# A transformer trunk on one Trainium2 core: the token sums of the seven-product pairs traced earlier, their bank evacuations at high priority, and another division of the scratch buffers

## The chip, the core and the metric

The kernel runs on one core of a Trainium2 chip. The engines that matter here are TensorE (PE: matmuls, with its weight loads PEld), VectorE (DVE), ScalarE (ACT), GpSimd (POOL) and SyncE (SP), whose queue starts nearly all transfers. Each engine works through its own instructions in a fixed order and waits on semaphores for the others. The metric is the device time of one execution in microseconds (us), lower being better.

## What is computed

Two layers run over 256 tokens of width 1024, in fp32. Each layer is a feed-forward block, a mixer (differential attention beside an mLSTM) and another feed-forward block, each with RMSNorm before and after. So there are four feed-forward passes, here called pass 1 to 4.

```python
def _swiglu(h, w_in, w_out):
    gate, up = jnp.split(h @ w_in, 2, axis=-1)
    return (jax.nn.silu(gate) * up) @ w_out

def reference(x, ffn_w_in, ffn_w_out, norm_gains, mix_w_in, mix_w_out, da_lambda, ...):
    for l in range(DEPTH):
        g = norm_gains[l]
        h = _swiglu(_rmsnorm(x, g[0]), ffn_w_in[l, 0], ffn_w_out[l, 0])
        x = x + 0.5 * _rmsnorm(h, g[1])
        lam_init = 0.8 - 0.6 * math.exp(-0.3 * l)
        h = _mixer(_rmsnorm(x, g[2]), mix_w_in[l], mix_w_out[l], da_lambda[l], da_subln_g[l],
                   lam_init, ml_conv_w[l], ml_conv_b[l], ml_gate_b[l], ml_norm_g[l])
        x = x + _rmsnorm(h, g[3])
        h = _swiglu(_rmsnorm(x, g[4]), ffn_w_in[l, 1], ffn_w_out[l, 1])
        x = x + 0.5 * _rmsnorm(h, g[5])
    return x
```

The hidden width is 2816, `w_in` is 1024 x 5632 and `w_out` 2816 x 1024.

## The kernel before

**Three matmuls for one.** Every fp32 operand is split into a high part (a copy by ACT to a shorter type, `wh` in line 296, `hh` or `both` in line 624) and a low part (a subtraction by DVE, `wl` in line 297, `hl` or `both` in line 625). Each product is the sum of high x high, low x high and high x low. The weights come from memory in pieces of 1 MB (`wr`, a ring of three buffers, issued on SP) and each half piece is split by one ACT copy and one DVE subtraction of 128 x 1024, here called casts. The split halves stand in rings of seven (`wl`, `wh`), to which buffers of another pool are lent in the feed-forward passes.

**Chunks and steps.** A pass works on 11 chunks of 256 hidden columns. Chunks 0 and 1 come first; then `STEPS` gives the order of PE: `I2 O0 I3 O1 P4 O2 I6 O3 I7 O4 O5 P8 O6 O7 I10`. An `I` step multiplies the tokens by a chunk's gate and up columns. The result is taken out of its banks by `ffn_hidden`: ACT forms `sil`, DVE forms `h` (line 598), one instruction for each of the two token tiles. Then `ffn_planes` turns `h`: ACT writes `planes` (line 605), a transposing DMA on SP turns them (line 607), ACT writes `hT` (line 609), and `ffn_hilo` splits that into `hh` and `hl`. An `O` step multiplies this by the chunk's rows of `w_out`.

**Pairs.** A `P` step does two chunks at once with seven products in place of eight, after Strassen's manner (`pair`, from line 706). `product` (line 705) is 12 matmuls, and the seven come in the order P1 P5 P6 P7 P2 P3 P4. The operands are sums: `pair_blocks` adds weight pieces on DVE (line 314, tiles `wide` and `wr`) and casts 14 halves. `pair_tokens` adds token tiles on DVE (lines 344 to 352, ten instructions) and splits the four sums (`both`); this is done once in a pass, and P4 and P8 share the sums. The products land in four banks, b1 and b2 of the ring `pin`, b3 and b4 of the ring `ptr`, two banks each. The banks are emptied by `p1` (ACT, line 717), `u` (line 721), `v` (lines 723 and 724) and so on. P3 accumulates on b4, so it starts only when DVE has added b4 to `v` (line 724). P1 writes the bank that chunk 3's first evacuation `h` empties.

**What sets the order.** PE's order in the steps is the order in which the code is written. On DVE, ACT and SP a scheduler in the compiler orders the instructions: by when they become ready in its own model, by the place where they are written, and by a high priority where the code asks for one. It also honours the buffers: each name has a tag with a ring of so many buffers (`TAGS` and `t2`, lines 152 to 158), and an instruction that writes a new buffer waits until the ring's oldest is free. A name without an entry goes to the ring `k2` of four. Before, `u`, `v` and `sum` are in the ring `ev` of five, together with `h`, `planes`, `turned` and `hT`; `sil` and `p1` are in `k2`.

Of the kernel before, what the change touches and what calls it, by code (L numbers as in the profile page):

```python
# [20 lines left out]
AF = mybir.ActivationFunctionType  # L21
ALU = mybir.AluOpType
# [3 lines left out]
P = 128  # L26
# [11 lines left out]
END = (8, 9, 10)  # L38
# [97 lines left out]
class _Trunk:  # L136
# [12 lines left out]
        return f"{s}_{self.n}"  # L149


    TAGS = {"kwn": ("kwn", 1), "aT0": ("aT0", 1), "aT1": ("aT1", 1)}
    for _n in ("nat", "ra", "rb", "rv", "tmp", "y", "so", "xg", "h", "planes", "turned", "hT", "u", "v", "sum"):
        TAGS[_n] = ("ev", 5)

    def t2(self, nm, shape=(P, 512), dt=F32):
        tag, bufs = self.TAGS.get(nm, ("k2", 4))
        return self.k2.tile(list(shape), dt, tag=tag, bufs=bufs, name=self.name(nm))
# [502 lines left out]
    def ffn(self, pre, gi_post):  # L661
        xT, r = pre

        def in_piece(t, kh, pin, w):
            xh, xl = xT[t][kh]
            for k in range(4):
                self.mm3(pin, xh[:, k, :], xl[:, k, :], *self.cols(w, k),
                         start=kh == 0 and k == 0, stop=kh == 1 and k == 3)
# [33 lines left out]
        def product(b, x, w, new):  # L702
            for k in range(4):
                for n, (st, mv) in enumerate(((x[0], 0), (x[0], 1), (x[1], 0))):
                    self.nc.tensor.matmul(b, st[:, k, :], self.cols(w, k)[mv], start=new and k == n == 0,  # L705
                                          stop=k == 3 and n == 2, skip_group_check=True)

        def pair(c):


            tt, stt = self.nc.vector.tensor_tensor, self.nc.vector.scalar_tensor_tensor
            w = self.pair_blocks()
            b1, b2, b3, b4 = self.bank_pin(), self.bank_pin(), self.bank_tr(), self.bank_tr()
            s1, s2, s3, s4 = sums
            product(b1, xT[0][0], w["P1"], True)
            p1 = self.t2("p1")
            self.nc.scalar.activation(p1, b1, AF.Copy)
            product(b4, s1, w["P5"], True)
            product(b2, s2, w["P6"], True)
            u, v, h0, sil = self.t2("u"), self.t2("v"), self.t2("h"), self.t2("sil")  # L720
            tt(u, b2, p1, op=ALU.subtract)
            product(b3, s3, w["P7"], True)
            tt(v, u, b3, op=ALU.subtract)
            tt(v, v, b4, op=ALU.add)
            product(b1, xT[0][1], w["P2"], False)
            self.func(sil, b1, AF.Silu, scale=r[0])
            product(b4, s4, w["P3"], False)
            tt(h0, b4, u, op=ALU.add)
            stt(h0, h0, r[0], sil, op0=ALU.mult, op1=ALU.mult)
            hT = [self.ffn_planes(h0)]  # L730
            product(b3, xT[1][1], w["P4"], False)
            tt(u, b3, u, op=ALU.subtract)
            self.func(u, u, AF.Silu, scale=r[1])
            stt(v, v, r[1], u, op0=ALU.mult, op1=ALU.mult)
            hT.append(self.ffn_planes(v))
            for j in range(2):
                hs[c + j] = self.ffn_split([h[:, j] for h in hT])

        hs, po = {}, []
# [20 lines left out]
        else:  # L760
# [6 lines left out]
            h = self.t2("h", (P, NT, 256))  # L767
# [12 lines left out]
            h = self.t2("h", (P, NT, 256))  # L780
# [3 lines left out]
            self.ffn_hidden(pb1, r[1], h[:, 1])  # L784
            hs[1] = ready(h)
        with self.tc.manual_schedule(engines={mybir.EngineType.PE}):
            both, sums, swap = list(self.both), None, 0
            for step in STEPS[:-1]:
                c = int(step[1:])
                if step[0] == "P":  # L790
                    sums = sums or self.pair_tokens(both)
                    pair(c)
                elif step[0] == "I":
                    if c == 3:
                        g = self.load_gpost(gi_post)
                        yield "middle"
                    ws = [self.piece(), self.piece()]
                    pins = [self.bank_pin() if swap else self.bank_tr() for _ in range(NT)]
                    swap = 1 - swap
                    for kh in range(2):  # L800
                        for t in range(NT):
                            in_piece(t, kh, pins[t], ws[kh])
                    chunk(c, pins)
                else:
                    if not po:
                        po = [[self.bank_bk() for _ in range(2)] for _ in range(NT)]
                    wo = self.piece()
                    for t in range(NT):
                        out_part(c, t, hs[c], wo)
            ws = [self.piece(), self.piece()]  # L810
            rows = self.token_scales(r)
            last = [self.piece() for _ in END[:-1]]
            banks = [[self.bank_pin() for _ in range(2)], [self.bank_tr() for _ in range(2)]]
            in_turned(banks, ws, both)

        yield "ending"
        hs[END[-1]] = self.ffn_turned(banks, rows)
        last.append(self.piece())
        for c, wo in zip(END, last):
            out_part(c, 0, hs[c], wo)  # L820
# [63 lines left out]
class _Mixer:  # L884
# [325 lines left out]
    def scores(self, t, h0):  # L1210

        tr, nc = self.tr, self.tr.nc
        nk, nh = P * (t + 1), 4 // (t + 1)
        if h0 == 0:
            self.aT[t] = tr.t2(f"aT{t}", (P, t + 1, 4, P))
            self.mx = tr.small("mx", (P, 2, 4))
            self.lsum[t] = tr.small("lsum", (P, 2, 4))
        hs = slice(h0, h0 + nh)
        pcs = [tr.bank_bk((P, nh, nk)) for _ in range(2)]
        for h in range(nh):  # L1220
            for c in range(2):
                rows = slice(c * 64, c * 64 + 64)
                self.mm(pcs[c][:, h, :], self.qkT[0][rows, h0 + h, t * P:(t + 1) * P],
                        self.qkT[1][rows, h0 + h, 0:nk], start=True, stop=True)
        for c in range(2):
            nc.vector.memset(pcs[c][0:64, :, nk - 64:nk], BIG)
            nc.vector.tensor_reduce(self.mx[:, c, hs], pcs[c], axis=AX.X, op=ALU.max, negate=True)
        if t:
            p = [tr.t2("p", (P, 2, nk)) for _ in range(nh)]
        else:  # L1230
            ts = [tr.t2("p", (P, 2, 2, nk)) for _ in range(nh // 2)]
            p = [ts[h // 2][:, h % 2] for h in range(nh)]
        self.p[t, h0] = p
        for h in range(nh):
            for c in range(2):
                tr.func(p[h][:, c, :], pcs[c][:, h, :], AF.Exp, bias=self.mx[:, c, h0 + h:h0 + h + 1],
                                accum_out=self.lsum[t][:, c, h0 + h:h0 + h + 1])

    def combine(self, t, h0):

        tr, nc, l = self.tr, self.tr.nc, self.l
        nk, nh = P * (t + 1), 4 // (t + 1)
        hs = slice(h0, h0 + nh)
        lsum, aT = self.lsum[t], self.aT[t]
        c1 = tr.small("c1", (P, nh))
        nc.vector.reciprocal(c1, lsum[:, 1, hs])
        self.stt(c1, c1, tr.neglam[:, l:l + 1], lsum[:, 0, hs], op0=ALU.mult, op1=ALU.mult)
        ptr = tr.bank_tr((P, t + 1, nh, P))
        for h in range(nh):
            p = self.p[t, h0][h]  # L1250
            self.stt(p[:, 0, :], p[:, 1, :], c1[:, h:h + 1], p[:, 0, :], op0=ALU.mult, op1=ALU.add)
            for kt in range(t + 1):
                self.T(ptr[:, kt, h, :], p[:, 0, kt * P:(kt + 1) * P], tr.ident)
        self.act(aT[:, :, hs, :], ptr, AF.Copy)

    def attend(self, t):
        tr, l = self.tr, self.l
        po = tr.bank_bk((P, 4, P))
        for h in range(4):
            for kt in range(t + 1):  # L1260
                self.mm(po[:, h, :], self.aT[t][:, kt, h, :], self.vd[:, kt, h * P:(h + 1) * P],
                        start=kt == 0, stop=kt == t)
        ss = tr.small("ssa", (P, 4))
        for h in range(4):
            self.act(tr.junk_tile(P), po[:, h, :], AF.Square, scale=2.0 ** -3.5, accum_out=ss[:, h:h + 1])
        l2 = tr.small("l2", (P, 4))
        self.tt(l2, self.lsum[t][:, 0, :], self.lsum[t][:, 0, :], op=ALU.mult)
        self.stt(ss, l2, EPS, ss, op0=ALU.mult, op1=ALU.add)
        sc = tr.rsqrt(ss, 4)
        y = tr.t2("y", (P, 4, P))  # L1270
        self.tt(y, po, sc.unsqueeze(2).broadcast_to([P, 4, P]), op=ALU.mult)
        self.y[t] = y
# [113 lines left out]
```

## Time and profile before

| what | value |
|---|---|
| time, median of three runs | 1002.9 us (1002.49 to 1003.31) |
| the profiled execution's own time | 1002.96 us |
| its span in the trace | 1001.2 us |
| mean granted clock of PE | 0.98 |
| weight casts on DVE from pieces / from sums | 324, 387.8 us / 48, 57.9 us |
| weight casts on ACT from pieces / from sums | 324, 335.0 us / 48, 50.4 us |
| transposing DMAs | 40, median 4.0 us from issue to landing |
| weight pieces of 1 MB | 162, median 4.8 us from issue to landing |

The feed-forward passes take about 0 to 197, 307 to 508, 508 to 700 and 812 to 1001 us of the span, the mixers what lies between. Here is what PE and the others did in these six stretches; the columns are the stretch, its length, the busy time and instructions of PE, PEld, DVE, ACT and POOL, then the granted clock of PE, the share of the DMA engines' time, and what they moved.

```profile
0.00:197.00 197.00, 181.65 (x801) 147.24 (x802) 156.02 (x206) 137.69 (x193) 6.97 (x22) 0.97 0.67 229
197.00:307.00 110.00, 108.01 (x595) 89.19 (x595) 86.33 (x163) 76.82 (x164) 7.42 (x10) 1.00 0.42 149
307.00:508.00 201.00, 192.02 (x859) 157.97 (x858) 162.54 (x203) 136.62 (x187) 2.73 (x5) 0.98 0.58 194
508.00:700.00 192.00, 179.51 (x794) 147.49 (x793) 151.39 (x185) 128.21 (x166) 2.17 (x4) 0.96 0.58 197
700.00:812.00 112.00, 112.00 (x613) 92.77 (x612) 90.10 (x165) 78.47 (x169) 7.28 (x11) 1.00 0.42 156
812.00:1001.20 189.20, 173.60 (x773) 142.73 (x771) 144.42 (x178) 121.20 (x155) 1.79 (x4) 0.97 0.52 178
```

PE has no idle time in the second mixer and 2 us in the first; what it lacks, it lacks in the feed-forward passes. In the rows of the trace, `a<-b` is the tile written and the tile read, and a bracket is the engine's idle time before the instruction and what ended it. Consecutive instructions of one kind can stand in one row, with their count.

### The profile page before, as it was taken

To read this page: it belongs to the slowest core of one execution; us is meant where nothing else is said; L and a number is where in the kernel's file an instruction comes from. 1 tells how busy PE (TensorE), PEld (TensorE's weight loads), DVE (VectorE), ACT (ScalarE), POOL (GpSimd) and SP (SyncE) were. 2 spreads that over 40 slices of the span, in tenths; PEclk is the share of its full clock that TensorE was granted. 3 is DMA by queue.
4 is the path that set the end of the run, shared out by engine and by line. 5 is a ranking of instruction groups with operands and counts; after the bars stand their busy time and mean duration, and the time that the engine had idled before them with its cause. 6 is when DMAs were issued, how large, how long until landed. Compare 5 with 4: busy or idle time off the path is not lost.

```text
span 1001.2 us, 12171 instructions
## 1 busy us (share of the span) xinstructions
PE 946.8 (95%) x4427; PEld 777.4 (78%) x4427; DVE 790.8 (79%) x1097; ACT 679.0 (68%) x1033; POOL 28.4 (3%) x55
## 2 busy tenths in 40 slices
PE   9969999999999989999999699999999999789997
PEld 7847887787788867887788578787888888678786
DVE  6799697689767799697578978867898587988854
ACT  7866776477765776776477666764778467676762
POOL 2000000000010000000000000000000100000000
PEclk9989999999999998999999799999999999899999
DMA  8955748335352845748347365582364348465541
GB/s 322 338 142 212 221 165 277 122 127 194 128 205 85 304 157 207 226 172 274 132 186 245 137 220 189 179 272 85 133 235 158 128 166 287 157 219 190 179 147 43
DMA packets 69882, 189.34 MB, mean 189 GB/s; under 512 B 45274, under 2 KB 46426, under 8 KB 49086
## 3 DMA queue, kind: packets, MB, share of 16 engines
q1 hardware_dynamic: 69246, 187.95, 54.8%
q8 instruction: 35, 0.57, 0.2%
q10 hardware_dynamic: 576, 0.61, 0.2%
q14 instruction: 25, 0.20, 0.1%
HBM read 177.01 MB, written 1.05 MB: 178 GB/s over the span
## 4 chain that ended last, share of the span: by engine, by line
PE 70%; DVE 14%; ACT 8%; DMA 5%; issue 3%; SPq 0%; POOLq 0%; DVEq 0%; ACTq 0%
PE ptr L705 8%; PE bk L471 8%; PE bk L473 8%; PE bk L472 8%; PE pin L471 7%; PE pin L473 7%; PE pin L472 7%; DVE wl L297 6%; PE pin L705 4%; ACT wh L296 3%; DMA turned<-planes 3%; PE ptr L471 2%; PE ptr L473 2%; PE ptr L472 2%; DMA wr<-in_w_dram 2%
## 5 line engine op out<-in xcount | busy, mean ns | idle before, releaser
L297 DVE TENSOR_TENSOR wl<-wr,wh 128x1024 fp32r<-128x1024 f32 x324 | 387.8, 1220 | 99.7 <-ACT wh L296 98.7
L296 ACT ACTIVATE wh<-wr 128x1024 fp32r<-128x1024 f32 x324 | 335.0, 1055 | 89.1 <-PE bk L473 21.1
L471 PE MATMUL pin<-wh,both 128*128 128x512 f32 x432 | 171.4, 398 | 0.0
L473 PE MATMUL pin<-wh,both 128*128 128x512 f32 x432 | 168.5, 390 | 0.0
L472 PE MATMUL pin<-wl,both 128*128 128x512 f32 x432 | 168.4, 390 | 0.0
L471 PE MATMUL bk<-wh,hh 128*128 128x512 f32 x352 | 137.6, 391 | 4.7 <-ACT hh L624 4.7
L472 PE MATMUL bk<-wl,hh 128*128 128x512 f32 x352 | 137.0, 389 | 0.0
L473 PE MATMUL bk<-wh,hl 128*128 128x512 f32 x352 | 137.0, 389 | 0.0
L705 PE MATMUL ptr<-wh,both 128*128 128x512 f32 x256 | 92.3, 428 | 40.4 <-ACT both L624 27.4
L705 PEld LDWEIGHTS ptr<-wh,both 128*128 128x128 f32 x256 | 52.4, 206 | 57.7 <-ACT both L624 29.1
L473 PEld LDWEIGHTS pin<-wh,both 128*128 128x128 f32 x432 | 81.1, 188 | 17.4
L471 PEld LDWEIGHTS pin<-wh,both 128*128 128x128 f32 x432 | 81.3, 188 | 17.0 <-issue 0.7
L472 PEld LDWEIGHTS pin<-wl,both 128*128 128x128 f32 x432 | 81.2, 188 | 15.6
L471 PEld LDWEIGHTS bk<-wh,hh 128*128 128x128 f32 x352 | 66.1, 188 | 19.4 <-ACT hh L624 6.0
L609 ACT ACTIVATE hT<-turned 128x1024 uint16<-128x1024 uint16 x40 | 54.7, 1369 | 32.9 <-DMA turned<-planes 32.8
L473 PEld LDWEIGHTS bk<-wh,hl 128*128 128x128 f32 x352 | 66.1, 188 | 13.8
L472 PEld LDWEIGHTS bk<-wl,hh 128*128 128x128 f32 x352 | 66.1, 188 | 13.4
L296 ACT ACTIVATE wh<-wide 128x1024 fp32r<-128x1024 f32 x48 | 50.4, 1055 | 22.7 <-DVE wide L314 14.1
L705 PE MATMUL pin<-wh,both 128*128 128x512 f32 x192 | 63.7, 393 | 0.0
L297 DVE TENSOR_TENSOR wl<-wide,wh 128x1024 fp32r<-128x1024 f32 x48 | 57.9, 1218 | 0.7
L705 PE MATMUL ptr<-wl,both 128*128 128x512 f32 x128 | 53.8, 420 | 0.0
L471 PE MATMUL ptr<-wh,both 128*128 128x512 f32 x128 | 49.8, 389 | 0.0
(242 smaller groups left out, 1360.4 us busy)
## 6 DMA issues: line engine op xcount, KB each, us to landing
wr<-in_w_dram SPq DMA_DIRECT2D x162, 1024.0 KB, 4.8
gpost<-in_gpost_dram SPq DMA_DIRECT2D x6, 512.0 KB, 6.3
wr<-in_w_dram SPq DMA_DIRECT2D x2, 512.0 KB, 5.5
wr<-in_w_dram SPq DMA_DIRECT2D x3, 256.0 KB, 4.3
x<-in_x_dram SPq DMA_DIRECT2D x3, 256.0 KB, 4.6
turned<-planes SPq DMA_TRANSPOSE x40, 4.0
out_dram<-x SPq DMA_DIRECT2D x2, 256.0 KB, 2.1
x<-in_x_dram SPq DMA_DIRECT2D x2, 128.0 KB, 2.8
```

The lines of the kernel that those rows point to most:

```text
L296: ia = nc.scalar.activation(hi, raw, AF.Copy)
L297: iv = nc.vector.tensor_tensor(lo, raw, hi.bitcast(F32), op=ALU.subtract)
L471: mm(ps, xh, wh, start=start, stop=False)
L472: mm(ps, xh, wl, start=False, stop=False)
L473: mm(ps, xl, wh, start=False, stop=stop)
L609: nc.scalar.activation(hT.rearrange("p a b n -> p (a b n)").bitcast(U16).rearrange("p (n u) -> p u n", u=2), turned.rearrange("p (u b) n - ...
L705: self.nc.tensor.matmul(b, st[:, k, :], self.cols(w, k)[mv], start=new and k == n == 0, stop=k == 3 and n == 2, skip_group_check=True)
```

## The change

Four things change. (1) `pair_tokens` is called ahead of the loop over the steps, so in front of step I2, and no longer just before P4. (2) The tiles `p1`, `sil`, `u`, `v` and `h` of a pair are taken when the pair begins, and the pair's evacuations, and the evacuation of the last chunk (`ffn_turned`), are written under a high priority. (3) `u`, `v` and `sum` leave the ring `ev`, which grows from five to eight, and so fall to the ring `k2` of four, with `sil` and `p1`. (4) The mixer's attention tile `aT` loses its own two buffers: it is taken from `ev` in one or two pieces, and copied out in one or two ACT instructions instead of one.

```diff
-    TAGS = {"kwn": ("kwn", 1), "aT0": ("aT0", 1), "aT1": ("aT1", 1)}
-    for _n in ("nat", "ra", "rb", "rv", "tmp", "y", "so", "xg", "h", "planes", "turned", "hT", "u", "v", "sum"):
-        TAGS[_n] = ("ev", 5)
+    TAGS = {"kwn": ("kwn", 1)}
+    for _n in ("nat", "ra", "rb", "rv", "tmp", "y", "so", "xg", "h", "planes", "turned", "hT", "aT"):
+        TAGS[_n] = ("ev", 8)
...
+            ahead = self.tc.high_priority
+            p1, sil, u, v, h0 = self.t2("p1"), self.t2("sil"), self.t2("u"), self.t2("v"), self.t2("h")
             product(b1, xT[0][0], w["P1"], True)
-            p1 = self.t2("p1")
-            self.nc.scalar.activation(p1, b1, AF.Copy)
+            with ahead():
+                self.nc.scalar.activation(p1, b1, AF.Copy)
             product(b4, s1, w["P5"], True)
             product(b2, s2, w["P6"], True)
-            u, v, h0, sil = self.t2("u"), self.t2("v"), self.t2("h"), self.t2("sil")
-            tt(u, b2, p1, op=ALU.subtract)
+            with ahead():
+                tt(u, b2, p1, op=ALU.subtract)
             product(b3, s3, w["P7"], True)
-            tt(v, u, b3, op=ALU.subtract)
-            tt(v, v, b4, op=ALU.add)
+            with ahead():
+                tt(v, u, b3, op=ALU.subtract)
+                tt(v, v, b4, op=ALU.add)
...
-            both, sums, swap = list(self.both), None, 0
+            both, swap = list(self.both), 0
+            sums = self.pair_tokens(both)
             for step in STEPS[:-1]:
                 c = int(step[1:])
                 if step[0] == "P":
-                    sums = sums or self.pair_tokens(both)
                     pair(c)
...
-        hs[END[-1]] = self.ffn_turned(banks, rows)
+        with self.tc.high_priority():
+            hs[END[-1]] = self.ffn_turned(banks, rows)
...
-            self.aT[t] = tr.t2(f"aT{t}", (P, t + 1, 4, P))
+            self.aT[t] = [tr.t2("aT", (P, 4, P)) for _ in range(t + 1)]
...
-        self.act(aT[:, :, hs, :], ptr, AF.Copy)
+        for kt in range(t + 1):
+            self.act(aT[kt][:, hs, :], ptr[:, kt], AF.Copy)
```

The lines of the pair move down with it: `p1` from 717 to 719, `u` from 721 to 723, `v` from 723 and 724 to 726 and 727. PE's order stays, but for the tiles of `aT`. Three places show what the scheduler makes of the rest.

First, DVE in pass 1, between the casts for chunk 2 (`wl_91` before, `wl_99` after) and the split of chunk 0; `h_57` is chunk 1's evacuation. Before:

```order
L297 TENSOR_TENSOR wl_91_496<-wr_6_494,wh_92_497 128x1024
L297 TENSOR_TENSOR wl_93_500<-wr_6_494,wh_94_501 128x1024
L205 TENSOR_TENSOR c_wgc_537<-c_1_530,c_wgc_537 128x16x8
L225 TENSOR_REDUCE c_hot_555<-c_0_95 100x4
L598 SCALAR_TENSOR_TENSOR h_57_376<-pin_55_326,rs1_31_274,sil_58_377 128x256
L598 SCALAR_TENSOR_TENSOR h_57_376<-pin_56_327,rs1_36_283,sil_59_380 128x256
L239 CAST c_hotp_565<-c_hot_555 36x256
L625 TENSOR_TENSOR hl_44_299<-hT_42_296,hh_43_298 128x256
L625 TENSOR_TENSOR hl_46_301<-hT_42_296,hh_45_300 128x256
```

After:

```order
L297 TENSOR_TENSOR wl_99_522<-wr_6_520,wh_100_523 128x1024
L297 TENSOR_TENSOR wl_101_526<-wr_6_520,wh_102_527 128x1024
L344 TENSOR_TENSOR sum_69_401<-both_6_129,both_19_187 128x512
L345 TENSOR_TENSOR sum_70_402<-both_6_129,both_19_187 128x512
L205 TENSOR_TENSOR c_wgc_563<-c_1_556,c_wgc_563 128x16x8
L225 TENSOR_REDUCE c_hot_581<-c_0_95 100x4
L598 SCALAR_TENSOR_TENSOR h_57_376<-pin_55_326,rs1_31_274,sil_58_377 128x256
L598 SCALAR_TENSOR_TENSOR h_57_376<-pin_56_327,rs1_36_283,sil_59_380 128x256
L346 TENSOR_TENSOR sum_69_401<-sum_69_401,sum_70_402 128x512
L239 CAST c_hotp_591<-c_hot_581 36x256
L625 TENSOR_TENSOR hl_44_299<-hT_42_296,hh_43_298 128x256
```

The first token sums stand among these rows now; before they stood some forty rows further on, behind the pair's casts for P2.

Second, DVE in pass 2, ahead of P1 of the pair P4. `h_678` before and `h_687` after are the two evacuations of chunk 3, the first of which empties the bank that P1 writes; `wl_713` and the other `wl` are casts for the pair. Before:

```order
L314 TENSOR_TENSOR wide_704_3434<-wide_704_3434,wr_61_3445 128x1024 x2
L625 TENSOR_TENSOR hl_656_3224<-hT_654_3221,hh_655_3223 128x256
L625 TENSOR_TENSOR hl_658_3226<-hT_654_3221,hh_657_3225 128x256
L297 TENSOR_TENSOR wl_709_3449<-wide_704_3434,wh_710_3450 128x1024
L598 SCALAR_TENSOR_TENSOR h_678_3341<-pin_676_3291,rs1_589_2926,sil_679_3342 128x256
L297 TENSOR_TENSOR wl_711_3453<-wide_704_3434,wh_712_3454 128x1024
L314 TENSOR_TENSOR wide_704_3434<-wide_704_3434,wr_62_3467 128x1024
L297 TENSOR_TENSOR wl_713_3459<-wr_60_3424,wh_714_3460 128x1024
L598 SCALAR_TENSOR_TENSOR h_678_3341<-pin_677_3292,rs1_614_3013,sil_680_3345 128x256
```

After:

```order
L297 TENSOR_TENSOR wl_710_3452<-wide_705_3437,wh_711_3453 128x1024
L297 TENSOR_TENSOR wl_714_3462<-wr_60_3427,wh_715_3463 128x1024
L297 TENSOR_TENSOR wl_716_3466<-wr_60_3427,wh_717_3467 128x1024
L314 TENSOR_TENSOR wide_705_3437<-wide_705_3437,wr_62_3470 128x1024
L297 TENSOR_TENSOR wl_712_3456<-wide_705_3437,wh_713_3457 128x1024
L297 TENSOR_TENSOR wl_720_3476<-wr_62_3470,wh_721_3477 128x1024
L297 TENSOR_TENSOR wl_718_3472<-wr_62_3470,wh_719_3473 128x1024
L314 TENSOR_TENSOR wide_705_3437<-wide_705_3437,wr_62_3470 128x1024
L598 SCALAR_TENSOR_TENSOR h_687_3370<-pin_685_3320,rs1_590_2929,sil_688_3371 128x256
L598 SCALAR_TENSOR_TENSOR h_687_3370<-pin_686_3321,rs1_615_3016,sil_689_3374 128x256
```

The evacuation stands behind all of the casts for P5, P6, P7 and P2 now, where before it stood in front of half of them.

Third, ACT at the same place: `planes_681` and `hT_683` before, `planes_690` and `hT_692` after, are chunk 3's, between which lies the transposing DMA. `planes_661` and `hT_663` are chunk 2's. `wh_722` and `wh_724` before and `wh_723` and `wh_725` after are the casts for P3. Before:

```order
L605 ACTIVATE planes_681_3348<-h_678_3341 128x1024
L296 ACTIVATE wh_718_3470<-wr_62_3467 128x1024
L296 ACTIVATE wh_720_3474<-wr_62_3467 128x1024
L296 ACTIVATE wh_722_3478<-wr_61_3445 128x1024
L609 ACTIVATE hT_683_3352<-turned_682_3350 128x2x512
L296 ACTIVATE wh_724_3482<-wr_61_3445 128x1024
L717 ACTIVATE p1_733_3511<-pin_729_3495 128x512
```

After:

```order
L605 ACTIVATE planes_661_3246<-h_658_3239 128x1024
L296 ACTIVATE wh_719_3473<-wr_62_3470 128x1024
L609 ACTIVATE hT_663_3250<-turned_662_3248 128x2x512
L624 ACTIVATE hh_664_3252<-hT_663_3250 128x256
L624 ACTIVATE hh_666_3254<-hT_663_3250 128x256
L605 ACTIVATE planes_690_3377<-h_687_3370 128x1024
L296 ACTIVATE wh_723_3481<-wr_61_3448 128x1024
L609 ACTIVATE hT_692_3381<-turned_691_3379 128x2x512
L719 ACTIVATE p1_734_3502<-pin_730_3498 128x512
L296 ACTIVATE wh_725_3485<-wr_61_3448 128x1024
```

Before, three casts stood between the planes and their `hT`; now only one stands there, chunk 2's turn comes between as well, and the last cast for P3 comes behind both.

More of the change, by code (lines that the diff above doesn't have):

```diff
@@ L714, in pair @@
             s1, s2, s3, s4 = sums
+            ahead = self.tc.high_priority
+            p1, sil, u, v, h0 = self.t2("p1"), self.t2("sil"), self.t2("u"), self.t2("v"), self.t2("h")
             product(b1, xT[0][0], w["P1"], True)
-            p1 = self.t2("p1")
-            self.nc.scalar.activation(p1, b1, AF.Copy)
+            with ahead():
+                self.nc.scalar.activation(p1, b1, AF.Copy)
             product(b4, s1, w["P5"], True)
             product(b2, s2, w["P6"], True)
-            u, v, h0, sil = self.t2("u"), self.t2("v"), self.t2("h"), self.t2("sil")
-            tt(u, b2, p1, op=ALU.subtract)
+            with ahead():
+                tt(u, b2, p1, op=ALU.subtract)
             product(b3, s3, w["P7"], True)
-            tt(v, u, b3, op=ALU.subtract)
-            tt(v, v, b4, op=ALU.add)
+            with ahead():
+                tt(v, u, b3, op=ALU.subtract)
+                tt(v, v, b4, op=ALU.add)
             product(b1, xT[0][1], w["P2"], False)
-            self.func(sil, b1, AF.Silu, scale=r[0])
+            with ahead():
+                self.func(sil, b1, AF.Silu, scale=r[0])
             product(b4, s4, w["P3"], False)
-            tt(h0, b4, u, op=ALU.add)
-            stt(h0, h0, r[0], sil, op0=ALU.mult, op1=ALU.mult)
+            with ahead():
+                tt(h0, b4, u, op=ALU.add)
+                stt(h0, h0, r[0], sil, op0=ALU.mult, op1=ALU.mult)
             hT = [self.ffn_planes(h0)]
             product(b3, xT[1][1], w["P4"], False)
-            tt(u, b3, u, op=ALU.subtract)
-            self.func(u, u, AF.Silu, scale=r[1])
-            stt(v, v, r[1], u, op0=ALU.mult, op1=ALU.mult)
+            with ahead():
+                tt(u, b3, u, op=ALU.subtract)
+                self.func(u, u, AF.Silu, scale=r[1])
+                stt(v, v, r[1], u, op0=ALU.mult, op1=ALU.mult)
             hT.append(self.ffn_planes(v))
@@ L1260, in attend @@
             for kt in range(t + 1):
-                self.mm(po[:, h, :], self.aT[t][:, kt, h, :], self.vd[:, kt, h * P:(h + 1) * P],
+                self.mm(po[:, h, :], self.aT[t][kt][:, h, :], self.vd[:, kt, h * P:(h + 1) * P],
                         start=kt == 0, stop=kt == t)
```

## The prediction

> **What bounds the kernel now.** First the page's totals and the chain that ended last, then the waits of TensorE (PE), then its timeline around the largest of them.
>
> ```profile
> span 1001.2 us, 12171 instructions
> PE 946.8 (95%) x4427; PEld 777.4 (78%) x4427; DVE 790.8 (79%) x1097; ACT 679.0 (68%) x1033; POOL 28.4 (3%) x55
> PE 70%; DVE 14%; ACT 8%; DMA 5%; issue 3%; SPq 0%; POOLq 0%; DVEq 0%; ACTq 0%
> ```
>
> PE is busy for 95% of the span, so all that a new order can win lies in the rest and in the matmuls that run slowly after a gap.
>
> ```profile
> PE ptr L705 <- ACT both L624: 27.4, 4, 9.8
> PE ptr L705 <- DVE v L724: 11.4, 8, 3.0
> PE bk L471 <- ACT hh L624: 4.7, 3, 1.7
> PE ptr L705 <- DVE both L625: 1.6, 1, 1.6
> ```
>
> The first row: four times, once in each pass, PE waits for the split token sums that product P5 multiplies (27.4 us; the last row is one more wait for a low half of theirs). The second: before product P3 it waits until VectorE (DVE) has taken P7 and P5 out of their banks (`v`, 11.4 us in eight waits). Here are these waits in the four P4 pairs, in order of time; the bracket is PE's idle time and what ended it.
>
> ```profile
> 74.57 0.79 PE L705 MATMUL ptr<-wh,both 128*128 128x512 f32 x1 [9.77 <-ACT both L624]
> ...
> 90.58 0.50 PE L705 MATMUL ptr<-wh,both 128*128 128x512 f32 x1 [2.36 <-DVE v L724]
> ...
> 375.47 0.50 PE L705 MATMUL ptr<-wh,both 128*128 128x512 f32 x1 [4.04 <-ACT both L624]
> ...
> 392.04 0.50 PE L705 MATMUL ptr<-wh,both 128*128 128x512 f32 x1 [0.79 <-DVE v L724]
> ...
> 569.01 0.80 PE L705 MATMUL ptr<-wh,both 128*128 128x512 f32 x1 [8.04 <-ACT both L624]
> ...
> 585.17 0.79 PE L705 MATMUL ptr<-wh,both 128*128 128x512 f32 x1 [2.30 <-DVE v L724]
> ...
> 870.83 0.79 PE L705 MATMUL ptr<-wh,both 128*128 128x512 f32 x1 [5.60 <-ACT both L624]
> ...
> 886.99 0.50 PE L705 MATMUL ptr<-wh,both 128*128 128x512 f32 x1 [2.98 <-DVE v L724]
> ```
>
> In each pair the sums' wait is followed 16 us later by a wait for DVE. So the sums are not what sets the pair's length: DVE is. Its busy time from chunk 1's evacuation (chunk 0's weights in pass 1) to P3's start confirms it; the columns are the stretch, its length, DVE's busy time and instructions, then the granted clock and the DMA.
>
> ```profile
> 31.26:90.53 59.27, 54.55 (x71) 0.91 0.64 214
> 338.58:391.99 53.41, 49.93 (x63) 0.94 0.54 177
> 528.57:585.12 56.55, 51.25 (x64) 0.91 0.53 173
> 832.15:886.93 54.78, 51.20 (x64) 0.94 0.54 180
> ```
>
> DVE idles for only 4.72, 3.48, 5.30 and 3.58 us there. **The start of P3 (90.58, 392.04, 585.17, 886.99) is my marker:** what moves it moves the rest of the pass, as PE has work without a gap behind it.
>
> **The change part by part.** The number of instructions on PE, SP and POOL stays. ACT gets four more `aT` copies over both mixers; before there were six:
>
> ```profile
> L1254 ACT ACTIVATE aT<-ptr x6: 577/582/612, 262.9 to 771.0; 128x512 f32<-128x512 f32 x6
> ```
>
> At most 4 x 0.6 = 2.4 us if nothing covered them; no PE wait above names `aT` and ACT is busy for 68%, so I take 0. The P8 pairs and the endings keep their DVE order, and I take 0 (within 1 us) for them too: their waits are what remains of the 11.4, and the 4.7. "Evacuations above casts" changes little: in the changed order casts still stand between `u`, `v` and `v` of the P4 pairs.
>
> *Sums earlier.* The ten sum instructions and four low halves move into the stretch ahead of chunk 2 or 3. DVE does the same work before P3, so it can gain only its idle time.
>
> In **pass 1** the sums fill the idle time and chunk 3's evacuation keeps its place among the casts. P3 then comes up to 4.72 us sooner, at 85.9. I take -4.7 (0 is the other end).
>
> In **passes 2 to 4** a second thing happens. `sil`, `sum`, `p1`, `u` and `v` now share one ring of four buffers. Chunk 3's `sil` waits for the sums' buffers, and its evacuation `h` falls behind all of the casts and adds for P5, P6, P7 and P2. P1 needs the bank that this `h` empties. The prices:
>
> ```profile
> 322.79 6.91 DVE L297 TENSOR_TENSOR wl<-wr,wh 128x1024 fp32r<-128x1024 f32 x6 [0.25 <-ACT wh L296]
> ...
> 379.01 0.69 DVE L344 TENSOR_TENSOR sum<-both 128x512 f32<-128x512 f32 x1
> 379.61 0.69 DVE L345 TENSOR_TENSOR sum<-both 128x512 f32<-128x512 f32 x1
> ...
> 341.55 0.75 DVE L625 TENSOR_TENSOR hl<-hT,hh 128x256 fp32r<-128x256 f32 x2
> ...
> 338.58 0.48 DVE L598 SCALAR_TENSOR_TENSOR h<-pin,rs,sil 128x256 f32<-128x256 f32 x1
> ...
> 528.57 0.48 DVE L598 SCALAR_TENSOR_TENSOR h<-pin,rs,sil 128x256 f32<-128x256 f32 x1
> ...
> 832.15 0.48 DVE L598 SCALAR_TENSOR_TENSOR h<-pin,rs,sil 128x256 f32<-128x256 f32 x1
> ```
>
> Back to back, six casts take 6.91 us: 1.14 each (the 128x1024 adds I price alike). A sum starts 0.60 after the one before. A low half takes about 0.34, an `h` 0.40. In the changed order 22 casts and adds, 14 sum instructions, 4 low halves and 3 `h` stand between chunk 1's `h` and chunk 3's: 25.0 + 8.4 + 1.3 + 1.2 = 36.0 us (rounded). With 0 to 3 us idle (from the 3.5 to 5.3 of the whole window; I take 1.5), from 0.40 behind the last three rows chunk 3's evacuation starts at E = 376.5, 566.5 and 870.05. P1 stood here:
>
> ```profile
> 368.55 0.39 PE L705 MATMUL pin<-wh,both 128*128 128x512 f32 x1
> ...
> 558.09 0.39 PE L705 MATMUL pin<-wh,both 128*128 128x512 f32 x1
> ...
> 862.35 0.39 PE L705 MATMUL pin<-wh,both 128*128 128x512 f32 x1
> ```
>
> So **PE waits about 8 us at P1** in place of the 4 to 8 at P5. This alone would cost little. But ACT works in order, and its new order has chunk 3's `hT` ahead of the cast `wh` for P3's second half. DVE needs that one next, so it stands still while the planes go through the transposing DMA:
>
> ```profile
> 344.08 1.05 ACT L605 ACTIVATE planes<-h 128x1024 uint16<-128x1024 uint16 x1
> ...
> 350.31 1.38 ACT L609 ACTIVATE hT<-turned 128x1024 uint16<-128x1024 uint16 x1 [1.90 <-DMA turned<-planes]
> ...
> 845.42 1.04 ACT L605 ACTIVATE planes<-h 128x1024 uint16<-128x1024 uint16 x1
> ...
> 849.26 1.39 ACT L609 ACTIVATE hT<-turned 128x1024 uint16<-128x1024 uint16 x1 [0.90 <-DMA turned<-planes]
> ...
> 372.38 1.03 ACT L296 ACTIVATE wh<-wr 128x1024 fp32r<-128x1024 f32 x1
> 373.31 0.58 ACT L717 ACTIVATE p<-pin 128x512 f32<-128x512 f32 x1
> ```
>
> From the planes' end to `hT` it is 5.2 and 2.8 us. On SP a weight piece of the next steps now goes ahead of this transposition, so I take 5.2 in pass 2 and 4.2 in the others. From E: two `h` 0.8, planes 1.0, transposition, `hT` 1.35, `p1` 0.55, `wh` 1.0; then on DVE eight casts (9.1), two low halves (0.7) and three evacuations (1.8), 11.55 in all. P3 starts at E + 21.4 in pass 2 and E + 20.4 in the others: 398, 587 and 890.5, that is **+5.9, +1.8 and +3.5**. The markers sum to -4.7 + 11.2 = +6.5 us.
>
> *Restarts.* After a gap PE is slower for a while:
>
> ```profile
> 569.01 5.51 PE ptr L705 x12
> 577.43 2.72 PE ptr L705 x12
> 585.17 7.25 PE ptr L705 x24
> 886.99 5.74 PE ptr L705 x24
> ```
>
> After 8.04 us the twelve matmuls of a product took 5.51 instead of 2.72; after 2.30 us the next 24 took 7.25, 1.8 more than two products; after 2.98 only 0.3 more. Before, only pass 3 paid at P3. In the changed kernel PE gets to P3 too early: in pass 1 by some 7 us (five products from 61.9, less a short wait at P6); in passes 2 to 4 five products and a restart take 16 us from P1, and P3 is ready 19.6 to 20.6 after it, a gap of 3.5 to 4.5. I take +2.0 in passes 1 and 2, +1.0 in pass 4, 0 in pass 3 (paid before): **+5.0**, bounds 0 and 8.
>
> [...]
>
> The profiled execution took 1002.96 us, the median is 1002.9, so no correction is needed: 1002.96 + 6.5 + 5.0 = 1014.5; I say **1015**. Ends: less idle -4.5, shortest transposition -5.2, no restart -5.0 gives 1000; more idle +4.5, longer transposition +2, all restarts +3, gives 1024, and up to 4.7 more if pass 1 wins nothing.
>
> **The rivals.** (1) *Faster, because the late evacuation is covered.* If the planes were turned by the time DVE needs P3's last cast, DVE would not stop. P3 would then come no sooner than P1's delay allows: E without idle + 0.8 + five products (13.6), plus up to 2.5 for the restart: 389.4 to 391.9, 579.4 to 581.9, 883 to 885.5. With -4.7 in pass 1 and the restart terms that is 986 to 994, say **990**. It decides at DVE's idle time in front of that cast: I expect some 6 us a pass, and below about 3.5 the change wins. For it speaks the 2.8 us transposition; against it ACT's order, with two in-line `hT` in front of the cast. 13%.
>
> (2) *No change.* DVE without idle before E and short transpositions: the markers sum to -3.3, the restarts give 3 to 6 back: **1003**. The 3.5 to 5.3 us of idle speak against it. 13%.
>
> (3) *The change does all that its words say*: the sums' wait and most restarts go and nothing comes in their place, 27.4 + 1.6, and 11 for four restarts of 2.8 (5.51 - 2.72): about **963**. Against it: the same DVE work lies ahead of P3. 3%.
>
> **How the numbers follow.** My forecast, slower, has 71%. A measurement of this kernel can tell 0.2%, 2 us, from no change. Faster 13 + 3 = 16%, same 13%, slower 71%. The range takes in the bounds and rival 2 and leaves out rivals 1 and 3 and a small tail above: 998 to 1027.
>
> **What would show it.** Right: no wait `both L624` at P5; a new PE wait of about 8 us at P1 for DVE `h` in passes 2 to 4 and none in pass 1; DVE idle for 5 us or more behind ACT `wh` or DMA `turned` ahead of P3; `v` waits of 3 to 7 us in all four pairs, with slow matmuls behind them. Wrong: chunk 3's `h` before 372 in pass 2, or an `hT` that waits for nothing; then it goes rival 1's way. P3 in pass 1 later than 90 would take away the only gain.

## The result, and the profile after

The changed kernel takes **1014.86 us** (median of four runs, 1014.10 to 1015.16) where the kernel before takes 1003.11 us (1002.49 to 1005.24 in four): a ratio of 1.0112 with a 95% interval of 1.0095 to 1.013. It is slower, by about 11 us. First the page's totals of the changed kernel.

```profile
span 1012.2 us, 12151 instructions
PE 950.0 (94%) x4427; PEld 780.0 (77%) x4427; DVE 789.3 (78%) x1097; ACT 675.1 (67%) x1037; POOL 28.5 (3%) x55
```

The span has grown by 11.0 us and PE's busy time by 3.2 us, though it runs the same matmuls: more of them run at a lower clock (the mean granted clock is 0.976 instead of 0.980). Next, PE's waits in the changed kernel: us in total, times, longest.

```profile
PE ptr L705 <- DVE v L727: 22.4, 8, 5.3
PE pin L705 <- DVE h L598: 22.3, 3, 7.9
```

The wait for the sums (27.4 and 1.6 us) is gone. In its place stand 22.3 us at P1 for chunk 3's evacuation, once in each of passes 2 to 4, and the waits for `v` have doubled from 11.4 to 22.4 us. The chain of work shows where the time came in. Here are the 24 matmuls of the products P3 and P4 in all eight pairs of the changed kernel (start, length); rows of the pair P4 and of the pair P8 take turns.

```profile
87.41 7.31 PE ptr L705 x24
...
152.65 5.78 PE ptr L705 x24
...
394.75 7.22 PE ptr L705 x24
...
459.90 5.73 PE ptr L705 x24
...
590.55 8.24 PE ptr L705 x24
...
656.58 5.76 PE ptr L705 x24
...
896.57 7.23 PE ptr L705 x24
...
961.58 5.76 PE ptr L705 x24
```

And of the kernel before, from the same view, the rows that have not been shown yet:

```profile
90.58 5.78 PE ptr L705 x24
...
154.28 5.73 PE ptr L705 x24
...
392.04 5.74 PE ptr L705 x24
...
455.70 5.74 PE ptr L705 x24
...
650.19 5.73 PE ptr L705 x24
...
950.50 5.74 PE ptr L705 x24
```

Each pass's share is the shift of its P8 pair less that of the pass before: -1.6, +5.8, +2.2 and +4.7 us. Within a pass P3 of the P4 pair moves by -3.2, +4.3, +1.2 and +3.2, and the rest is its 24 matmuls, which take 7.2 to 8.2 us instead of 5.7 (7.25 in pass 3).

What happens ahead of P3 is seen on DVE in pass 2 of the changed kernel. The first row is the first instruction of chunk 1's evacuation, the second the first of the sums, the third chunk 3's evacuation; then come the rows with idle time, and `u` and `v`.

```profile
337.14 0.48 DVE L598 SCALAR_TENSOR_TENSOR h<-pin,rs,sil 128x256 f32<-128x256 f32 x1
337.54 0.68 DVE L344 TENSOR_TENSOR sum<-both,both 128x512 f32<-128x512 f32 x1
...
373.84 0.89 DVE L598 SCALAR_TENSOR_TENSOR h<-pin,rs,sil 128x256 f32<-128x256 f32 x2
376.30 0.76 DVE L625 TENSOR_TENSOR hl<-hT,hh 128x256 fp32r<-128x256 f32 x2 [1.57 <-ACT hh L624]
378.51 1.23 DVE L297 TENSOR_TENSOR wl<-wr,wh 128x1024 fp32r<-128x1024 f32 x1 [1.45 <-ACT wh L296]
383.06 1.23 DVE L297 TENSOR_TENSOR wl<-wr,wh 128x1024 fp32r<-128x1024 f32 x1 [3.32 <-ACT wh L296]
...
388.27 0.69 DVE L723 TENSOR_TENSOR u<-pin,p 128x512 f32<-128x512 f32 x1
...
391.14 0.69 DVE L726 TENSOR_TENSOR v<-u,ptr 128x512 f32<-128x512 f32 x1
...
394.01 0.69 DVE L727 TENSOR_TENSOR v<-v,ptr 128x512 f32<-128x512 f32 x1
```

Behind the evacuation DVE stands still for 6.3 us in three pieces, each for ACT, and then works through casts between `u` and the two `v`. Why ACT was late is in the chain of work of the same stretch:

```profile
369.35 5.09 DMA turned<-planes
...
374.46 1.36 ACT hT L609
...
376.57 0.95 ACT planes L605
...
377.55 2.71 DMA turned<-planes
...
380.27 1.36 ACT hT L609
...
381.97 1.06 ACT wh L296
```

In pass 2 two transpositions, chunk 2's and then chunk 3's, stand in ACT's line, and the cast that DVE needs next comes behind both. In passes 3 and 4 it is chunk 3's alone: chunk 2's `hT` starts at 566.72 and 871.79, ahead of chunk 3's evacuation at 569.48 and 875.49. From the end of chunk 3's planes to its `hT` it is 4.6 us there, and DVE stands still for 6.6 us in each of these passes, in two pieces for ACT's casts.

### The profile page after: what moved, and what is told of

It reads as the page before. It is cut to its first block, busy times and chain, and to the rows that moved or that the text cites. A ratio compares the mean times of both kernels' runs of the same rounds, so it can differ in the third digit from the quotient of the medians.

```text
span 1012.2 us, 12151 instructions
## 1 busy us (share of the span) xinstructions
PE 950.0 (94%) x4427; PEld 780.0 (77%) x4427; DVE 789.3 (78%) x1097; ACT 675.1 (67%) x1037; POOL 28.5 (3%) x55
## 4 chain that ended last, share of the span: by engine, by line
PE 71%; DVE 16%; ACT 6%; DMA 4%; issue 3%; SPq 0%; DVEq 0%; POOLq 0%; ACTq 0%
PE bk L471 8%; PE bk L472 8%; PE bk L473 8%; DVE wl L297 8%; PE ptr L705 7%; PE pin L471 7%; PE pin L473 7%; PE pin L472 7%; PE pin L705 3%; DMA turned<-planes 3%; PE ptr L471 2%; PE ptr L473 2%; PE ptr L472 2%; ACT wh L296 2%; DVE wide L314 2%
## 5 line engine op out<-in xcount | busy, mean ns | idle before, releaser
L471 PE MATMUL pin<-wh,both 128*128 128x512 f32 x432 | 171.5, 398 | 0.0
L473 PE MATMUL pin<-wh,both 128*128 128x512 f32 x432 | 168.5, 390 | 0.0
L705 PE MATMUL ptr<-wh,both 128*128 128x512 f32 x256 | 89.7, 418 | 22.4 <-DVE v L727 22.4
L473 PEld LDWEIGHTS pin<-wh,both 128*128 128x128 f32 x432 | 81.1, 188 | 17.3
L471 PEld LDWEIGHTS pin<-wh,both 128*128 128x128 f32 x432 | 81.3, 188 | 17.0 <-issue 0.7
L705 PE MATMUL pin<-wh,both 128*128 128x512 f32 x192 | 68.3, 417 | 23.3 <-DVE h L598 22.3
L705 PEld LDWEIGHTS pin<-wh,both 128*128 128x128 f32 x192 | 38.9, 203 | 33.3 <-issue 23.5
```

Of the source, the lines that this page charges most:

```text
L471: mm(ps, xh, wh, start=start, stop=False)
L473: mm(ps, xl, wh, start=False, stop=stop)
```

## The experiments

Three theories were held against each other. **A**: the sums, traced early, hold the buffers that chunk 3's `sil` needs; its evacuation falls behind the pair's casts, its turning lands in ACT's line in front of P3's last cast, and DVE then reaches `v` late, through casts that are not needed yet. **B**: the new division of the scratch buffers costs the time by itself. **C**: the high priority does. All ratios below are to the kernel before, run on the same chip beside it; the medians are of four runs, of ten for all_but_early, turn_behind and evac_first.

| kernel | us, median | ratio, 95% interval |
|---|---|---|
| early_only | 1025.68 | 1.0215 [1.0178, 1.0252] |
| all_but_early | 1004.42 | 1.0001 [0.9986, 1.0015] |
| turn_behind | 1009.09 | 1.0047 [1.0028, 1.0066] |
| evac_first | 1005.42 | 1.0014 [1.0001, 1.0026] |
| no_priority | 1011.39 | 1.0085 [1.0058, 1.0111] |
| v_ahead | 982.55 | 0.9794 [0.9769, 0.9819] |
| three_orders | 973.01 | 0.9704 [0.9675, 0.9734] |
| sil_apart | 961.77 | 0.9588 [0.9562, 0.9614] |
| before_v_ahead | 986.37 | 0.9828 [0.9808, 0.9849] |
| sil_only | 989.04 | 0.9853 [0.983, 0.9877] |

**Which part costs the time.** The kernel before with the early call alone (early_only), and the changed kernel without it (all_but_early):

```diff
-            both, sums, swap = list(self.both), None, 0
+            both, swap = list(self.both), 0
+            sums = self.pair_tokens(both)
...
-                    sums = sums or self.pair_tokens(both)
```

> The kernel before, with the token sums traced ahead of the steps and nothing else: the old buffers (sums in the ring of five with h and hT), no high priority. Theory A (the early sums push chunk 3's evacuation behind the pair's casts and bring its turning DMA in front of P3's last cast): the order still has both in passes 2 to 4, so PE waits for DVE h at P1 for 6 to 9 us there, and the time is 1010 to 1016 us. Theory B (the new division of the scratch buffers costs the time): 1001 to 1005, no wait at P1. Theory C (the high priority costs it): the same as B.

> The changed kernel with the token sums traced in front of P4 again; buffers and priorities as changed. Theory A: no wait at P1, the sums' wait at P5 is back (20 to 28 us in all), u and v stand about one cast earlier than before, and the time is 996 to 1003 us. Theory B or C: 1010 to 1016 us, since what costs the time is still in.

PE's wait at P1, in early_only:

```profile
PE pin L705 <- DVE h L598: 34.2, 4, 11.1
```

and its waits for the sums, in all_but_early:

```profile
PE ptr L705 <- DVE both L625: 21.4, 8, 5.8
PE ptr L705 <- ACT both L624: 7.5, 8, 2.9
```

B and C fall: all but the early call changes nothing that can be measured (its 1004.42 us lie 1.4 above the range given), and the early call alone brings the wait at P1. But A's number for early_only was missed by 10 us. With the old buffers the evacuation is later still (P1 waits 10 to 11 us, and 2.7 us in pass 1). By the code, the sums there fill the ring of five in which `h` itself and `hT` live; that this is why it came later was not tested. So the early call alone costs some 22 us, and the rest of the change, which does nothing alone, gives half of that back. By no_priority below it is not the priority that does so, which leaves the new division of the buffers, or the place at which the pair's tiles are taken.

**The priority.** The changed kernel without it:

```diff
-            ahead = self.tc.high_priority
+            import contextlib
+            ahead = contextlib.nullcontext
...
-        with self.tc.high_priority():
+        if True:
             hs[END[-1]] = self.ffn_turned(banks, rows)
```

> The changed kernel without any high priority (the pair's evacuations and the last chunk's are written at the normal one). If the priority does what its words say, u and v now wait behind more casts, and the time is over 1017 us. If it decides nothing (DVE's order ahead of P3 stays as it was, cast for cast): 1013 to 1017 us, waits at P1 and P3 unchanged within 1 us.

1011.39 us, 1.6 us below the range of the second case, with an interval that overlaps that of the changed kernel. P1 waits 7.4, 7.9 and 7.2 us, as in the changed kernel. The `v` waits are 18.6 us instead of 22.4; in pass 2 that at P3 is 3.3 instead of 5.0, with one cast instead of two between the two `v`, so not all waits stayed within the 1 us of the second case. The high priority doesn't bring the evacuations above the casts, and nothing is won by it here; whether it costs some 3 us is not settled. Why the scheduler gives it so little weight was not looked into.

**The turn in ACT's line.** Chunk 3's hidden tile is kept until the pair has its weights, and its `hT` is ordered behind P3's last cast (`held` is an empty list at the start, `turn` and `cast3` are the two ACT instructions):

```diff
             for t in range(NT):
                 self.ffn_hidden(pins[t], r[t], h[:, t])
-            hs[c] = ready(h)
+            if c == 3:
+                held.append(h)
+            else:
+                hs[c] = ready(h)
...
             w = self.pair_blocks()
+            if held:
+                hs[3] = ready(held.pop())
+                self.after(self.turn, [self.cast3])
```

> The changed kernel, but chunk 3's hidden tile is turned inside the pair, and ACT's hT of it stands behind the last cast for P3 (an order on ACT alone; chunk 2's hT stays in line). Theory A: the wait at P1 stays at 7 to 8 us, DVE's idle time ahead of P3 falls by some 3.3 us in passes 2 to 4, P3 comes 3 to 3.5 us sooner in each, the v waits there fall below 2.3 us and most of their restarts (about 1.8 us) go: 1000 to 1006 us. A rival by which the late evacuation alone sets P3 (PE needs its 16 us from P1): 1011 to 1015 us.

**The place of the evacuation.** The casts for P6 behind chunk 3's evacuation (`emptied` is its second instruction, and the fifth cast of the pair is the first for P6):

```diff
+            if c == 4:
+                assert not self.turns
+                self.turns = [[], [], [], [], [(None, self.emptied)]]
             w = self.pair_blocks()
```

> The changed kernel, with DVE's casts for P6 ordered behind chunk 3's evacuation, which moves 5 casts and adds behind it in pass 2 and 3 in passes 3 and 4. Theory A: the wait at P1 falls by 5.7 us in pass 2 and 3.4 us in passes 3 and 4, the turn begins as much sooner while DVE has casts to do, so its idle time ahead of P3 falls by 3 to 5 us a pass, and the time is 1000 to 1007 us. If the place of the evacuation doesn't matter (DVE's sum of work alone sets P3): 1012 to 1016 us.

PE's waits for `v` in turn_behind (line 710 is the product, 735 the second `v`; P1's wait stays):

```profile
PE ptr L710 <- DVE v L735: 17.0, 8, 5.3
```

and its wait at P1 in evac_first:

```profile
PE pin L705 <- DVE h L598: 13.3, 3, 4.8
```

Both gain, as A said and its rivals did not: the evacuation 9 us, within the range given, and the turn 6, less than the range. With the evacuation ordered first, P1's wait fell by 9.0 us, where A had 12.5, and the `v` waits hardly (20.8 us). With the turn out of the way the `v` waits in passes 2 to 4 were 3.6, 2.3 and 1.9 us instead of 5.0, 4.1 and 5.1. In pass 2 DVE's idle time behind the evacuation fell only from 6.3 to 5.0 us, where A had 3.3 less: chunk 2's turn stays, DVE then waited 1.6 us in smaller pieces for the casts on ACT, and it had three casts instead of two between `u` and `v`. Neither order alone makes the change pay.

**The casts in front of `v`.** The six casts after the pair ordered behind the second `v`, which is what the change's words say of evacuations and casts; once in the changed kernel (v_ahead) and once in the kernel before (before_v_ahead):

```diff
-                tt(v, v, b4, op=ALU.add)
+                iv = tt(v, v, b4, op=ALU.add)
...
                 hs[c + j] = self.ffn_split([h[:, j] for h in hT])
+            assert not self.turns
+            self.turns = [[(None, iv)]] * 6
```

> The changed kernel, with the six casts after the pair (chunk 2's w_out piece and chunk 6's first pieces) ordered on DVE behind v, the addition of b4: what the change's words promise, done by an order. Theory A (P3 waits for DVE's own row of casts, 5 of them not needed before P3): the v waits at P3 fall from 4 to 5.3 us to under 1.5 in all four P4 pairs, the restarts behind them go, P1's wait stays at 7 to 8; 5 to 6 us less in each pass, 990 to 997 us. If P3's time hangs on the turn in ACT's line instead: 1008 to 1015 us.

> The kernel before, with the six casts after the pair ordered on DVE behind v, and nothing of the change. Theory A: the v waits of P3 in the P4 pairs go (8.4 us) with pass 3's restart (1.8) and the P8 pairs' small waits (up to 2.9), the sums' wait stays at 27 to 29 us: 988 to 994 us, some 6 to 10 us above the changed kernel with the same order (982.55), in which only the late evacuation's 22 us remain. If the early sums are what made that order pay: 999 to 1003 us.

In v_ahead PE has no wait for `v` any more, in any of the eight pairs; the largest that is left is

```profile
PE pin L705 <- DVE h L598: 22.0, 3, 7.9
```

and DVE in pass 2 goes from `u` to the second `v` in 1.9 us, where it took 5.7:

```profile
376.95 0.69 DVE L723 TENSOR_TENSOR u<-pin,p 128x512 f32<-128x512 f32 x1
378.10 0.69 DVE L726 TENSOR_TENSOR v<-u,ptr 128x512 f32<-128x512 f32 x1 [0.47 <-PE ptr L705]
378.82 0.69 DVE L727 TENSOR_TENSOR v<-v,ptr 128x512 f32<-128x512 f32 x1
```

The gain was 32 us and not the 18 to 25 expected. The sum closes from the changed kernel's rows: the `v` waits 22.4, and the eight stretches of 24 matmuls took 53.0 us where without a gap ahead of them they take 43.5 (5.44 each, twice the 2.72 us of one product's 12 in the chain of work), so 9.5 more. I had left out the P8 pairs and taken the restarts too small. In the kernel before the same order gives 17 us (11.4 of `v` waits, 3.9 in the eight stretches of matmuls, 1.7 at the sums), 1.6 beyond the range given, and the wait that stays is the sums':

```profile
PE ptr L705 <- ACT both L624: 26.2, 4, 10.4
```

986.37 against 982.55: with `v` ahead, the change as a whole is worth 4 us (the intervals overlap), though PE still waits 22 us at P1 for the late evacuation.

**All orders, and the buffer.** three_orders has the last three edits in the changed kernel. sil_apart has those on `hT` and `v`, and instead of the order on the evacuation one name more in the ring of eight; sil_only has this name alone:

```diff
-    for _n in ("nat", "ra", "rb", "rv", "tmp", "y", "so", "xg", "h", "planes", "turned", "hT", "aT"):
+    for _n in ("nat", "ra", "rb", "rv", "tmp", "y", "so", "xg", "h", "planes", "turned", "hT", "aT", "sil"):
```

> The changed kernel with all three orders at once: P6's casts behind chunk 3's evacuation, chunk 3's hT behind P3's last cast, the casts after the pair behind v. Theory A: P1 waits 4 to 5 us, P3 under 1.5 us, and the time is 980 to 990 us, below that of both kernels. If the three gains are one gain seen three times: 990 to 998 us.

> The changed kernel with sil moved from the ring of four (which the sums fill) to the ring ev of eight, and the orders on hT and v of the run before; no order on the evacuation. Theory A (chunk 3's evacuation is late because its sil waits for a buffer that a sum holds): chunk 3's evacuation goes back among the casts by itself, the wait at P1 falls below 3 us, 975 to 988 us. If the evacuation is late for another reason (the sums' work itself): P1 waits 5 us or more, 985 to 995 us.

> The changed kernel with sil in the ring of eight, and nothing else (one name more in one line). Theory A: the wait at P1 falls from 22 us to under 6 in all, DVE's idle time behind chunk 3's turn mostly goes as the turn begins sooner, but P3 still stands behind DVE's casts, and the v waits grow to 5 to 8 us a pair: 994 to 1003 us, no slower than before. If the buffer isn't the reason: 1010 to 1016 us.

The wait at P1 in three_orders, and in sil_apart behind its waits for `v`:

```profile
PE pin L710 <- DVE h L600: 13.3, 3, 4.8
```

```profile
PE ptr L710 <- DVE v L735: 5.6, 3, 2.9
...
PE pin L710 <- DVE h L600: 4.3, 3, 1.8
```

In sil_only PE's wait at P1 is this, and DVE begins with the sums of pass 2 here:

```profile
PE pin L705 <- DVE h L598: 4.9, 3, 2.7
```

```profile
317.22 0.69 DVE L344 TENSOR_TENSOR sum<-both,both 128x512 f32<-128x512 f32 x1
```

In the changed kernel DVE had this stretch (its length, DVE's busy time and instructions, the clock, the DMA) ahead of chunk 1's evacuation:

```profile
307.00:337.14 30.14, 22.66 (x29) 1.00 0.62 220
```

The buffer is the reason: one name in a list turns the change from 11 us slower into 14 us faster than before, with P1's wait down from 22.3 to 4.9 us. But it does more than A said, and 989.04 us lie 5 below the range given. In the changed kernel the first sum of pass 2 comes at 337.5, behind chunk 1's evacuation; here it comes 20 us sooner (3.8 of them because pass 1 is shorter: P3 of its P8 pair starts at 148.90 instead of 152.65), in a stretch in which DVE has time: there it was idle for 7.5 of 30.1 us. So sums and `sil` seem to have held each other up in both directions, and the run doesn't separate the two effects. The `v` waits stay, at 23.4 us. **sil_apart, at 961.8 us, is 4.1% faster than before** and the fastest of all; all gains with `v` ahead came out larger than expected.

## Why the prediction was right

The forecast was 1015 us, slower; measured 1014.86. Step by step:

- *The sums' wait goes and a wait at P1 of about 8 us takes its place in passes 2 to 4, none in pass 1.* Right: 7.2, 7.9 and 7.2 us. That the shared ring of four is the reason is borne out by sil_only, where 4.9 us of this wait are left; the sums also come sooner there.
- *36.0 us of DVE work between chunk 1's and chunk 3's evacuation, and 1.5 us idle.* In pass 2 it was 36.3 us from 0.40 behind 337.14 to 373.84, nearly all work. The idle time was taken too long: measured against the shift of the pass before, the evacuation came 1.0 to 1.2 us sooner than forecast in all three passes.
- *From there 21.4 us to P3 in pass 2.* It was 20.9, but by luck, as two errors cancel. Chunk 2's turn, which I had named and not counted, held chunk 3's planes up by 1.8 us; the transposition behind them then took 2.7 us, not 5.2. In passes 3 and 4 it was 21.1 us, not 20.4: the transposition took 4.6, not 4.2.
- *Markers -4.7, +5.9, +1.8, +3.5, in all +6.5.* They were -3.2, +4.3, +1.2, +3.2: +5.5. In pass 1 the sums did not fill all of DVE's idle time:

```profile
31.26:87.36 56.10, 54.98 (x71) 0.97 0.69 231
```

  1.1 of 4.7 us stayed, and the same 71 instructions were busy for 0.4 us more.
- *Restarts +5.0.* They were +1.5, +1.5, +1.0 and +1.5, so 5.5: the size was right and pass 3, put at 0, paid too. With the markers that makes 11.0 us where 11.5 were forecast; that the whole fits so well is in part luck, as several terms were off by 1 to 2 us in both directions.
- *Nothing in the mixers, the P8 pairs, the endings; the priority and the four `aT` copies decide nothing.* Right in the main. From the P8 pair of one pass to P1 of the next the shift changes by 0.3 us at most, and PE's waits for `v` in the P8 pairs are 2.9 us in both kernels. Without the early call the priority and the copies change nothing (all_but_early, 1.0001); in the changed kernel the time without the priority is some 3 us shorter, with overlapping intervals (no_priority).
- *Rival 1, that the turn is covered:* DVE's idle time, put at 6 us a pass, was 6.3 in pass 2 and 6.6 in passes 3 and 4. *Rival 3, that the change does all that its words say,* was priced at 963 us; sil_apart, in which evacuation and `v` nearly stand where the words put them, takes 961.8. It gets there by explicit orders that the change does not have, and by a somewhat different sum: the `v` waits fell by 5.8 us to 5.6, and waits at P1 and P6 of 5.6 us came in.

Where the reasoning was too narrow: "DVE does the same work before P3, so it can gain only its idle time" holds for the order that the scheduler made. It hid that some casts before `v` need not be there (five in pass 2 of the changed kernel). To order the six after the pair behind `v` is worth 17 us in the kernel before and 32 in the changed one.

## What to carry to other kernels

When work is traced earlier, look first at what else draws on the same ring of buffers: an early producer holds them until its last reader, and what waits for them can be an evacuation that frees a bank. Count what stands in an engine's line between a wait and the instruction that releases it; here the high priority did not clear that line, and an explicit order did. And when one of two stalls goes, ask which other chain is about to be late at the same place: here the turn and the casts both stood between DVE and P3, and taking the turn out of ACT's line alone was worth 6 us, less than DVE had idled behind it, as other casts took its place.

## What the runs showed of the hardware

For gaps of 1.9 to 3.3 us the length did not tell whether PE slowed down. In turn_behind a gap of 1.89 us was followed by a slow stretch and one of 2.30 us was not (idle time in the bracket):

```profile
586.37 0.50 PE L710 MATMUL ptr<-wh,both 128*128 128x512 f32 x1 [2.30 <-DVE v L735]
...
888.25 0.50 PE L710 MATMUL ptr<-wh,both 128*128 128x512 f32 x1 [1.89 <-DVE v L735]
```

The 24 matmuls behind the gap of 2.30 us took 5.75 us, those behind the gap of 1.89 us 7.38. In the kernel before, a gap of 2.30 us was followed by a slow stretch (7.25 us); in no_priority one of 3.26 us at 394.15 was not (5.75). In these three and in evac_first, sil_apart, sil_only and the changed kernel, the nine gaps of 1.89 to 3.26 us at P3 were followed by a slow stretch (7.18 us and more) four times, and the sixteen gaps of 3.38 us and more (up to 6.96) each time (7.09 us and more). At 888.25 the slow stretch began only about 1 us after the restart: the stretch, its length, PE's busy time and matmuls, the granted clock, the DMA.

```profile
888.25:889.30 1.05, 1.05 (x5) 1.00 1.06 375
889.30:892.90 3.60, 3.60 (x10) 0.53 0.96 360
```

So at 888.25 the granted clock was 1.00 for the first microsecond and 0.53 for some 3.6 us, in which the matmuls came 0.43 us apart; from 892.93 on they came 0.23 us apart again, as in the first microsecond. What decides whether and when PE slows down was not shown. In the changed kernel the 24 matmuls behind a restart in the P4 pairs, behind gaps of 4.05 to 5.33 us, took 1.8 to 2.8 us more (7.22 to 8.24 against 5.44, at a granted clock of 0.67 to 0.78), the most behind the shortest gap; in the P8 pairs, behind 0.66 to 0.81 us, they took 0.3 more (5.73 to 5.78) at a granted clock of 1.00.
